# One stretch of whole-array products in each expert round, weights of the second block in pairs, and the next block's first chunk later in the queue

## The chip, the cores and the metric

The kernel runs on one core of one Trainium2 chip. The metric is the time of one execution on the device in microseconds (us), as the median of several runs; a lower time is better. The engines are named as in the profile: PE is the matrix engine (PEld its weight loads), DVE, ACT and POOL are the vector, scalar and general engines, and SP issues the DMA transfers.

## The reference

A sequence of 256 tokens of width 1024 goes through a first block of two layers and then a second block of one layer, all in 32-bit floating point. Of the first block, the part that matters here is the mixture of experts at the end of each layer: each token is sent to two of 32 experts, and each expert is a small gated network.

```python
def first_block(x, ...):
    for l in range(2):
        x = x + mixer(rms_norm(x, attn_norm[l])) @ w_out[l]       # mLSTM, attention, gating
        x = x + hier_moe(rms_norm(x, ffn_norm[l]), ..., w1[l], w3[l], w2[l])

def expert_block(rows, rw, e):              # inside hier_moe, for each expert e
    xi = x_pad[rows]                        # its tokens
    h = silu(xi @ w1[e]) * (xi @ w3[e])     # 1024 -> 256, twice
    return (h @ w2[e]) * rw                 # 256 -> 1024, added back to the tokens

def second_block(x, ...):
    proj = rms_norm_2(x, norm_w) @ w_in_2   # 1024 -> 6144: two attentions, gates
    ...
    return x + y @ w_out_2
```

## The kernel before

The 256 tokens stay in the core's memory; nearly all traffic is weights. A queue of weight tiles of 128 x 2048 (1 MB each) is written out by hand at L237 to L262, and SP issues it strictly in that order. A tile is issued when the program hands back a buffer (`done` at L214, which calls `pump` at L174). During the expert stage 19 buffers of other uses are lent to the queue, and at its end (`reclaim`, L201) only five remain.

An expert's weights are three tiles: "first thirds" and "second thirds" hold w1 and w3 for the two halves of the 1024 input features, and "third matrices" hold w2. The 32 experts are dealt with in 11 rounds: rounds 0, 1 and 4 to 7 have two experts of 64 token places each, the others four experts of 32 places. A round's products use the array in two or four column groups, one for each expert, which can run at the same time: `hidden` (L1127) has 8 steps, `outp` (L1163) has 4, and one step is one product for each of the round's experts. These are called tiled products below. Each of them stands in the trace as two records, since the data is 32-bit.

The other products of a round use the whole array of 128 columns: `gather` (L1108) picks the tokens of the next two rounds and scales them into X (32 products, evicted by ACT at L1122 through the two PSUM buffers called "a"; the two halves of one buffer hold two eviction groups of four products), `gates` (L1089), `turn` (L1146, the transposes of a round's hidden values and its place matrix) and `combine` (L1184, adds a round's output to the token sums, four products for each half n). `gather` and `gates` run in odd rounds, for the two rounds that follow.

Who follows whom in the program of round i: `hidden(i)`, in whose middle (`mid_way`, L1243) stand `combine(i-2, 1)` and `turn(i-1)`; then the two halves of `outp(i-1)`, and in odd rounds a half of the gather behind each of them (`prepare_four`, L1191). A planner turns the program into one order for each engine: at each moment of its own model of time it takes the earliest instruction of the program that is ready. So an instruction whose PSUM buffer or weights are late by that model is overtaken by later ones, and the order on PE in the trace is mixed.

At the end of a layer the first weight chunk of the next block stands eight places before the end of the layer's tiles (L254), ahead of the third matrices of rounds 9 and 10; it is split into a high and a low half by ACT and DVE (`prepare`, `split`, L266 to L274) after `hidden(10)`. The last four tiles arrive in halves (L189 to L197).

In the second block `tok512` (L1381) multiplies the tokens with 512 columns of weights as two chunks of 256 columns, each over all 1024 features: three products for each of 8 feature groups and 2 token groups (`tokm`, L470, and `mm3`, L457).

Of the kernel before, what the change touches and what calls it, by code (L numbers as in the profile page):

```python
# [45 lines left out]
for _c in W_IN_CHUNKS:  # L46
    W_IN_OFF.append(W_IN_OFF[-1] + _c)


# [58 lines left out]
def block_kernel(ctx: ExitStack, tc: tile.TileContext, A, out):  # L108
# [48 lines left out]
    def acc():  # L157
        return mm("acc")
# [78 lines left out]
    for l in range(L):  # L237
        ex = []
        rounds = [ROUNDS[i][1] for i in LOADS]
        for now, before in zip(rounds + [[]], [[]] + rounds):  # L240
            for c in range(2):
                ex.extend(chunk_of(l, e, c) for e in now)
            ex.extend(chunk_of(l, e, 2) for e in before)
        ex.insert(BRIEF, ex.pop(3))
        for i in range(len(W_IN_CHUNKS)):
            a, b = W_IN_OFF[i], W_IN_OFF[i + 1]
            if l == 0 or i:
                queue.append((("in", l, i), A["w_in"][l][:, 8 * a:8 * b]))
            if i == 1:
                queue.append((("u", l), A["w_u"][l]))  # L250
            if i in EARLY:
                queue.append(ex.pop(0))
        queue.extend((("out", l, i), A["w_out"][l][:, i * 2048:(i + 1) * 2048]) for i in range(4))
        ex.insert(len(ex) - 8, following(l + 1))  # L254
        queue.extend(ex)
# [228 lines left out]
    def chunks(key, k):  # L484

        prepare(key)
        i = split_keys.index(key) + 1
        if i < len(split_keys) and split_keys[i] in loaded and split_keys[i][:2] == key[:2]:
            prepare(split_keys[i])
        return [t.rearrange("p (k c) -> p k c", k=k) for t in ready.pop(key)]  # L490

    def mixer(l):
# [584 lines left out]
    def experts(l, xh, xl, whl, slot, wg, perms, P0, mci):  # L1077
# [29 lines left out]

        def gather(q, k2s=range(4)):  # L1108

            P = Ps[q]  # L1110
            n = P.shape[2]
            for k2 in k2s:
                ps = mm("a").rearrange("p (a b) -> p a b", a=2)
                for a in range(2):
                    k = 2 * k2 + a
                    i = 0
                    for t in (xh, xl):
                        for j in range(2):
                            nc.tensor.matmul(ps[:, a, :n], t[:, j, k * 128:(k + 1) * 128], P[:, j], start=i == 0,  # L1119
                                             stop=i == 3)  # L1120
                            i += 1
                    nc.scalar.activation(X[:, k, :n], ps[:, a, :n], AF.Identity, bias=0.0, scale=g[:, k:k + 1])  # L1122

        def keys(i):
            return [[("e", l, e, c) for c in range(3)] for e in ROUNDS[i][1]]

        def hidden(i, mid_way):  # L1127
            q, p = divmod(i, 2)
# [3 lines left out]
            for k in range(8):  # L1132
# [4 lines left out]
                if k == 3:  # L1137
                    done(*[x[0] for x in kk_])
                    mid_way()
            done(*[x[1] for x in kk_])  # L1140
# [21 lines left out]

        def outp(i, between):  # L1163
            nonlocal yhl
# [5 lines left out]
            for n in range(2):  # L1170
# [8 lines left out]
                if n:  # L1179
                    done(*[x[2] for x in kk_])  # L1180
                    combine(i, 0)
                between(n)

        def combine(i, n):  # L1184
            PT = hs[i][1]
            for t in range(2):
                for j in range(2):
                    nc.tensor.matmul(po[j][n], PT[:, j * 128:(j + 1) * 128], yhl[:, n, t],  # L1188
                                     start=i == 0 and t == 0, stop=i == NR - 1 and t == 1)

        def prepare_four(q, n):  # L1191
            if n:
                gates(q)
            gather(q, (2 * n, 2 * n + 1))

# [7 lines left out]
        warm(3)  # L1203
        prepare_four(0, 0)
        prepare_four(0, 1)

# [33 lines left out]
        for i in range(NR):  # L1240
            q, p = divmod(i, 2)
            last = 2 * q + 2 >= NR
            def mid_way():  # L1243
                if i > 1:
                    combine(i - 2, 1)
                if i:
                    turn(i - 1)
                (arrange_places, arrange_weights, lambda: None)[min(i, 2)]()
                if i == NR - 2:
                    add_plain()  # L1250

            hidden(i, mid_way)
            if i == NR - 1:
                reclaim()
                prepare(following(l + 1)[0])
                x = big("x", [128, 2, D], name="x")
            if p == 0 and not last:
                onehot(q + 1)
            if i:
                outp(i - 1, (lambda n: prepare_four(q + 1, n)) if p and not last else lambda n: None)  # L1260
        combine(NR - 2, 1)
        most = nc.values_load(mci[0:1, 0:1], min_val=0, max_val=1 << 14)
        tc.no_sync_barrier()
        tc.mark_branch_hint_location(f"fits{l}", hint=0, engines=[mybir.EngineType.PE])
        turn(NR - 1)
        outp(NR - 1, lambda n: None)
        take_x(po, 0)
# [95 lines left out]
    def second():  # L1363
# [17 lines left out]
        def tok512(i, dst):  # L1381
            for c in range(2):
                w = win2(i + c)
                ps = acc().rearrange("p (a b) -> p a b", a=2)
                tokm(ps, hT, w, 256)
                for j in range(2):
                    copy_scaled(dst[:, j, c * 256:(c + 1) * 256], ps[:, j], r[:, j:j + 1])

# [207 lines left out]
def pack(I):  # L1596
# [71 lines left out]
    A["vec2"] = v2  # L1668
    A["w_in_2"] = c(kp(f(I["w_in_2"])[0]).reshape(128, 8, 24, 256).transpose(2, 0, 1, 3).reshape(24, 128, 2048))
    for n, s in (("w_up_a", "w_up_moba_2"), ("w_up_b", "w_up_sb_2")):  # L1670
# [19 lines left out]
```

## Time and profile before

| | before |
|---|---|
| median of 3 runs | 961.7 us (960.76 to 962.31) |
| the profiled execution | 966.68 us, span 964.9 us |
| PE busy | 938.3 us, 97% of the span |
| expert stage of layer 0, of layer 1 (first gather to the last combine) | 154.8 to 376.5 us, 515.3 to 735.2 us |
| moved from memory | 271.27 MB read, 284 GB/s over the span |

The profile is of one execution; its span runs from the first to the last instruction. A busy PE says only that some product was in flight: a product on one column group alone counts like one on all four. DMA shares are of the core's 16 DMA engines.

### The profile page before, as it was taken

Reading aid. Unit: us, or ns where it says so; the run is one execution under the profiler, and the core shown is the slowest. Engines: PE = TensorE matmul, PEld = TensorE weight load, DVE = VectorE, ACT = ScalarE, POOL = GpSimd, SP = SyncE. Lnnn points to the kernel's source line nnn. Section 1 sums busy time; section 2 is a strip of 40 time slices with the busy share of each in tenths; the row PEclk is TensorE's granted clock in tenths of the full one; section 3 lists DMA queues with packets and bytes.
Section 4 is the critical chain, followed back from the end, with each engine's and each line's share of the span. In section 5 each row is a group of like instructions: output and inputs, shape, how many; then the busy total and the mean of one; then the engine's idle time right before and its main releaser. Section 6 shows DMA issues by size and latency. Waiting matters only on the chain.

```text
span 964.9 us, 14997 instructions
## 1 busy us (share of the span) xinstructions
PE 938.3 (97%) x5834; PEld 622.2 (64%) x5834; DVE 466.2 (48%) x1121; ACT 380.4 (39%) x714; POOL 20.3 (2%) x60
## 2 busy tenths in 40 slices
PE   8989999999999999999999999999998999999998
PEld 6878875433244335889885433344335988899996
DVE  5698665211111115688665211111115777786574
ACT  5576442212122015585542212122125446845442
POOL 0100000000000000300000000000000000000000
PEclk9999999999999999999999999999999999999999
DMA  9537467999999999437568899999999542155531
GB/s 355 181 131 288 160 256 286 369 367 420 421 422 420 397 418 366 126 133 283 185 236 303 352 392 422 420 420 421 416 418 365 181 155 102 45 175 177 186 119 43
DMA packets 42589, 273.38 MB, mean 283 GB/s; under 512 B 5256, under 2 KB 7440, under 8 KB 12048
## 3 DMA queue, kind: packets, MB, share of 16 engines
q1 hardware_dynamic: 40160, 268.48, 70.9%
q10 hardware_dynamic: 2352, 3.87, 1.3%
q8 instruction: 49, 0.80, 0.3%
q14 instruction: 28, 0.23, 0.1%
HBM read 271.27 MB, written 2.63 MB: 284 GB/s over the span
## 4 chain that ended last, share of the span: by engine, by line
PE 80%; DVE 7%; DMA 7%; ACT 5%; issue 1%; SPq 0%; DVEq 0%; ACTq 0%
PE mm L1135 18%; PE mm L459 10%; PE mm L460 10%; PE mm L461 10%; PE mm L1174 10%; PE mm L1119 6%; PE mm L1188 4%; DMA w<-in_w_e 3%; DMA w<-in_w_in 3%; DVE wlo L273 2%; ACT whi L272 1%; PE mm L571 1%; PE mm L576 1%; PE mm L689 1%; DMA x<-in_x 1%
## 5 line engine op out<-in xcount | busy, mean ns | idle before, releaser
L1135 PE MATMUL mm<-w,X 128*32 128x512 f32 (+1 forms) x1024 | 191.1, 598 | 2.0 <-DMA w<-in_w_e 2.0
L273 DVE TENSOR_TENSOR wlo<-w,whi 128x1024 fp32r<-128x1024 f32 (+3 forms) x124 | 145.3, 1183 | 26.4 <-ACT whi L272 26.3
L272 ACT ACTIVATE whi<-w 128x1024 fp32r<-128x1024 f32 (+3 forms) x124 | 122.2, 1016 | 72.8 <-issue 42.4
L1174 PE MATMUL mm<-w,ehT 128*32 128x512 f32 (+1 forms) x512 | 132.8, 600 | 1.0 <-ACT ehT L1158 1.0
L459 PE MATMUL mm<-hT,whi 128*128 128x256 f32 (+2 forms) x432 | 125.4, 290 | 0.2 <-ACT whi L272 0.2
L461 PE MATMUL mm<-hT,wlo 128*128 128x256 f32 (+2 forms) x432 | 124.6, 288 | 0.8 <-DVE wlo L273 0.8
L460 PE MATMUL mm<-lT,whi 128*128 128x256 f32 (+2 forms) x432 | 124.6, 288 | 0.0
L1135 PEld LDWEIGHTS mm<-w,X 128*32 128x32 f32 (+1 forms) x1024 | 48.2, 119 | 94.5 <-issue 83.6
L460 PE MATMUL mm<-wlo,hT 128*128 128x256 f32 x288 | 83.9, 291 | 1.1 <-DVE wlo L273 1.1
L459 PE MATMUL mm<-whi,hT 128*128 128x256 f32 x288 | 84.6, 294 | 0.1
L461 PE MATMUL mm<-whi,lT 128*128 128x256 f32 x288 | 83.5, 290 | 0.0
L459 PEld LDWEIGHTS mm<-hT,whi 128*128 128x128 f32 (+2 forms) x432 | 80.7, 187 | 2.3 <-issue 0.8
L460 PEld LDWEIGHTS mm<-lT,whi 128*128 128x128 f32 (+2 forms) x432 | 80.6, 187 | 1.8 <-issue 1.3
L461 PEld LDWEIGHTS mm<-hT,wlo 128*128 128x128 f32 (+2 forms) x432 | 80.6, 187 | 1.7 <-DVE wlo L273 1.5
L1122 ACT ACTIVATE X<-mm,vec 128x256 f32<-128x256 f32 (+1 forms) x96 | 43.3, 455 | 93.4 <-PE mm L1119 92.5
L1178 DVE TENSOR_TENSOR yhl<-mm,yhl 128x512 fp32r<-128x512 f32 x44 | 30.2, 691 | 90.1 <-ACT yhl L1177 90.1
L1174 PEld LDWEIGHTS mm<-w,ehT 128*32 128x32 f32 (+1 forms) x512 | 31.5, 119 | 61.9 <-issue 55.2
L1143 DVE SCALAR_TENSOR_TENSOR eh<-eh,mm 128x256 f32<-128x256 f32 x22 | 9.3, 421 | 108.0 <-ACT eh L1142 108.0
L1119 PEld LDWEIGHTS mm<-P,xh 128*128 128x128 f32 x192 | 29.3, 188 | 49.2 <-ACT X L1122 32.5
L1160 DVE TENSOR_SCALAR ePT<-mm,C 128x256 fp32r<-128x256 f32 x22 | 10.6, 484 | 100.8 <-ACT ehT L1158 100.8
L460 PEld LDWEIGHTS mm<-wlo,hT 128*128 128x128 f32 x288 | 55.5, 193 | 2.9 <-DVE wlo L273 1.5
L1142 ACT ACTIVATE eh<-mm,gt 128x256 f32<-128x256 f32 x22 | 10.4, 474 | 118.1 <-PE mm L1135 118.1
(460 smaller groups left out, 1485.2 us busy)
## 6 DMA issues: line engine op xcount, KB each, us to landing
w<-in_w_e SPq DMA_DIRECT2D x184, 1024.0 KB, 12.7
w<-in_w_in SPq DMA_DIRECT2D x37, 1024.0 KB, 4.9
w<-in_w_out SPq DMA_DIRECT2D x12, 1024.0 KB, 4.9
w<-in_w_e SPq DMA_DIRECT2D x16, 512.0 KB, 9.0
w<-in_w_in SPq DMA_DIRECT2D x4, 768.0 KB, 4.2
w<-in_w_up_a SPq DMA_DIRECT2D x2, 1024.0 KB, 4.8
w<-in_w_up_b SPq DMA_DIRECT2D x2, 1024.0 KB, 4.8
w<-in_w_u SPq DMA_DIRECT2D x2, 960.0 KB, 10.9
```

Of the source, the lines that this page charges most:

```text
L272: nc.scalar.activation(hi[:, s_], w[:, s_], AF.Copy)
L273: nc.vector.tensor_sub(lo[:, s_], w[:, s_], hi[:, s_].bitcast(F32))
L459: nc.tensor.matmul(ps, st[0], mv[0], start=first, stop=False)
L460: nc.tensor.matmul(ps, st[0], mv[1], start=False, stop=False)
L461: nc.tensor.matmul(ps, st[1], mv[0], start=False, stop=last)
L1119: nc.tensor.matmul(ps[:, a, :n], t[:, j, k * 128:(k + 1) * 128], P[:, j], start=i == 0, stop=i == 3)
L1122: nc.scalar.activation(X[:, k, :n], ps[:, a, :n], AF.Identity, bias=0.0, scale=g[:, k:k + 1])
L1135: nc.tensor.matmul(ph[w * a:w * a + w], X[:, k, c0:c0 + w], take(kk_[a][k // 4])[:, (k % 4) * 512:(k % 4 + 1) * 512], start=k == 0, stop=k ...
L1160: nc.vector.tensor_scalar(PT, pT[:, 256:], cc("place" if w == 64 else "place32"), None, op0=OP.is_equal)
L1174: nc.tensor.matmul(py[w * a:w * a + w], hT[:, c * 128 + w * a:c * 128 + w * a + w], take(kk_[a][2])[:, n * 1024 + c * 512:n * 1024 + (c + ...
L1178: nc.vector.tensor_sub(yhl[:, n, 1], py, yhl[:, n, 0].bitcast(F32))
L1188: nc.tensor.matmul(po[j][n], PT[:, j * 128:(j + 1) * 128], yhl[:, n, t], start=i == 0 and t == 0, stop=i == NR - 1 and t == 1)
```

## The change

In the expert stage, `mid_way` and `prepare_four` go. The program of round i becomes `hidden(i)` without an interruption, `outp(i-1)` without one, and then all whole-array products in one go: `combine(i-1, 0)` (inside `outp`), `turn(i)`, in odd rounds the whole of `gather` and `gates`, and `combine(i-1, 1)`. `gather` takes its PSUM buffers in turn from "b" and "a", four in all, and in all gathers but a layer's first the second half of each buffer is evicted by DVE in place of ACT. The queue takes the next block's first chunk four places from the end of the layer's tiles: behind the third matrices of round 9 and ahead of those of round 10. In the second block `tok_pair` takes two chunks as two halves of the features for all 512 columns, and each product is 512 columns wide, into two PSUM buffers.

```diff
-        ex.insert(len(ex) - 8, following(l + 1))
+        ex.insert(len(ex) - 4, following(l + 1))
...
+    def tok_pair(hT, first, second):
+        ps = [acc() for j in range(2)]
+        for half, key in enumerate((first, second)):
+            w = chunks(key, 4)
+            for k in range(4):
+                for j in range(2):
+                    mm3(ps[j], [t[:, 4 * half + k, j * 128:(j + 1) * 128] for t in hT], [t[:, k] for t in w],
+                        half == 0 and k == 0, half == 1 and k == 3)
+        return ps
...
-        def gather(q, k2s=range(4)):
+        def gather(q):
...
-            for k2 in k2s:
-                ps = mm("a").rearrange("p (a b) -> p a b", a=2)
+            for k2 in range(4):
+                ps = mm("baba"[k2]).rearrange("p (a b) -> p a b", a=2)
...
-                    nc.scalar.activation(X[:, k, :n], ps[:, a, :n], AF.Identity, bias=0.0, scale=g[:, k:k + 1])
+                    if a and q:
+                        nc.vector.tensor_scalar(X[:, k, :n], ps[:, a, :n], g[:, k:k + 1], None, op0=OP.mult)
+                    else:
+                        nc.scalar.activation(X[:, k, :n], ps[:, a, :n], AF.Identity, bias=0.0, scale=g[:, k:k + 1])
...
-            def mid_way():
-                if i > 1:
-                    combine(i - 2, 1)
-                if i:
-                    turn(i - 1)
-                (arrange_places, arrange_weights, lambda: None)[min(i, 2)]()
-                if i == NR - 2:
-                    add_plain()
-
-            hidden(i, mid_way)
+            hidden(i)
             if i == NR - 1:
                 reclaim()
                 prepare(following(l + 1)[0])
                 x = big("x", [128, 2, D], name="x")
+
+            if i:
+                outp(i - 1)
+            if i < NR - 1:
+                turn(i)
+            (arrange_places, arrange_weights, lambda: None)[min(i, 2)]()
             if p == 0 and not last:
                 onehot(q + 1)
+            if i == NR - 2:
+                add_plain()
+            if p and not last:
+                gather(q + 1)
+                gates(q + 1)
             if i:
-                outp(i - 1, (lambda n: prepare_four(q + 1, n)) if p and not last else lambda n: None)
-        combine(NR - 2, 1)
+                combine(i - 1, 1)
...
         def tok512(i, dst):
-            for c in range(2):
-                w = win2(i + c)
-                ps = acc().rearrange("p (a b) -> p a b", a=2)
-                tokm(ps, hT, w, 256)
-                for j in range(2):
-                    copy_scaled(dst[:, j, c * 256:(c + 1) * 256], ps[:, j], r[:, j:j + 1])
+            for j, ps in enumerate(tok_pair(hT, ("in2", i), ("in2", i + 1))):
+                copy_scaled(dst[:, j], ps, r[:, j:j + 1])
```

## Rows read from the trace of the kernel before

**Rows 1.** The page: slices of 24 us, granted PE clock and DMA share, in tenths

```profile
PEclk9999999999999999999999999999999999999999
DMA  9537467999999999437568899999999542155531
```

**Rows 2.** Windows, layer 0: stretch, length, busy PE, PEld, DVE, ACT, POOL, clock, DMA share, GB/s

```profile
182.00:192.00 10.00, 10.00 (x54) 5.51 (x52) 1.68 (x8) 3.32 (x8) 0.00 (x0) 1.00 0.92 344
192.00:198.00 6.00, 6.00 (x47) 2.27 (x50) 1.10 (x3) 0.86 (x2) 0.00 (x0) 1.00 0.52 171
...
215.00:310.00 95.00, 95.00 (x416) 38.19 (x409) 16.66 (x42) 20.76 (x42) 0.00 (x0) 1.00 1.01 421
310.00:325.00 15.00, 15.00 (x92) 4.56 (x90) 2.96 (x7) 2.31 (x5) 0.00 (x0) 1.00 0.96 376
```

**Rows 3.** Windows, layer 1, the same columns

```profile
545.00:553.00 8.00, 8.00 (x50) 4.49 (x52) 1.55 (x7) 2.75 (x6) 0.00 (x0) 1.00 0.85 295
553.00:560.00 7.00, 7.00 (x62) 2.47 (x54) 1.15 (x3) 0.54 (x2) 0.00 (x0) 1.00 0.69 238
```

**Rows 4.** Waits of SP's queue between 186 and 197 us: total, times, longest

```profile
SPq L191 <- PE mm L1135: 6.6, 1, 6.6
```

**Rows 5.** Timeline of PE, part of round 1: start, length, line, shapes, records

```profile
180.70 0.50 PE L1119 MATMUL mm<-P,xh 128*128 128x256 f32 x2
...
181.37 1.07 PE L1174 MATMUL mm<-w,ehT 128*64 128x512 f32 x2
182.37 0.51 PE L1119 MATMUL mm<-P,xh 128*128 128x256 f32 x2
...
183.51 1.08 PE L1174 MATMUL mm<-w,ehT 128*64 128x512 f32 x4
184.53 0.50 PE L1119 MATMUL mm<-P,xh 128*128 128x256 f32 x2
```

**Rows 6.** Waits of the engines over the whole span: total, times, longest

```profile
PEld mm L1119 <- ACT X L1122: 32.5, 44, 0.8
```

**Rows 7.** Timeline of PE, round 7, where nothing is gathered

```profile
282.99 3.60 PE L1174 MATMUL mm<-w,ehT 128*64 128x512 f32 x16
286.52 1.20 PE L1188 MATMUL mm<-yhl,ePT 128*128 128x512 f32 x4
287.65 3.65 PE L1135 MATMUL mm<-w,X 128*64 128x512 f32 x16
```

**Rows 8.** Timeline of PE: first and last of eleven tiled stretches before 194.0 us

```profile
158.09 1.07 PE L1135 MATMUL mm<-w,X 128*64 128x512 f32 x2
...
192.03 2.77 PE L1135 MATMUL mm<-w,X 128*32 128x512 f32 x22
```

**Rows 9.** Groups by line and shape: count, busy us, mean ns, idle before

```profile
L1122 ACT ACTIVATE X<-mm,vec 128x256 f32<-128x256 f32 x80 | 37.4, 473 | 73.4 <-PE mm L1119 72.5
```

**Rows 10.** SP's transfer of the next chunk at 334.8 us: issue, time to landing

```profile
L191 SPq DMA_DIRECT2D w<-in_w_in x1: 429/429/429, 334.8 to 334.8; - x1
...
DMA to landing us min/median/max: 16.7/16.7/16.7
```

**Rows 11.** Timeline, end of layer 0

```profile
363.00 1.99 ACT L272 ACTIVATE whi<-w 128x1024 fp32r<-128x1024 f32 x2
...
372.48 0.16 PEld L1174 LDWEIGHTS mm<-w,ehT 128*32 128x32 f32 x8 [0.93 <-SPq L1276]
```

**Rows 12.** Timeline of PE: products of 256 and of 512 columns, a wait in the second block

```profile
741.03 0.38 PE L448 MATMUL mm<-C,x 128*128 128x128 f32 x2 [1.75 <-DVE lT L455]
...
891.02 0.28 PE L459 MATMUL mm<-hT,whi 128*128 128x256 f32 x1
891.14 0.28 PE L460 MATMUL mm<-lT,whi 128*128 128x256 f32 x1
...
945.05 0.39 PE L459 MATMUL mm<-whi,yh 128*128 128x512 f32 x1
945.28 0.39 PE L460 MATMUL mm<-wlo,yh 128*128 128x512 f32 x1
```

**Rows 13.** Timeline of PE, round 9: the output products of four experts

```profile
337.80 1.04 PE L1174 MATMUL mm<-w,ehT 128*32 128x512 f32 x2
...
347.42 3.62 PE L1174 MATMUL mm<-w,ehT 128*32 128x512 f32 x20
```

More of the change, by code (lines that the diff above doesn't have):

```diff
@@ L47 @@
     W_IN_OFF.append(W_IN_OFF[-1] + _c)
+PAIRS, PAIRS2 = (2, 8), (0, 2, 4, 12)
 VC = dict(attn=0, ffn=8, mix=16, conv_w=24, conv_b=56, gate=64, aq=66, akv=68, qh=69, kh=70, bs=71)
@@ L1121, in gather, with hidden @@
                             i += 1
-                    nc.scalar.activation(X[:, k, :n], ps[:, a, :n], AF.Identity, bias=0.0, scale=g[:, k:k + 1])
+                    if a and q:
+                        nc.vector.tensor_scalar(X[:, k, :n], ps[:, a, :n], g[:, k:k + 1], None, op0=OP.mult)
+                    else:
+                        nc.scalar.activation(X[:, k, :n], ps[:, a, :n], AF.Identity, bias=0.0, scale=g[:, k:k + 1])
         def keys(i):
             return [[("e", l, e, c) for c in range(3)] for e in ROUNDS[i][1]]
-        def hidden(i, mid_way):
+        def hidden(i):
             q, p = divmod(i, 2)
@@ L1138, in hidden @@
                     done(*[x[0] for x in kk_])
-                    mid_way()
             done(*[x[1] for x in kk_])
@@ L1161, in turn, with outp @@
             hs[i] = hT, PT
-        def outp(i, between):
+        def outp(i):
             nonlocal yhl
@@ L1181, in outp @@
                     combine(i, 0)
-                between(n)
         def combine(i, n):
@@ L1189, in combine @@
                                      start=i == 0 and t == 0, stop=i == NR - 1 and t == 1)
[L1191 to L1194, printed above, removed]
         slotT = small([NE, 2, 256], BF, name="slotT")
@@ L1203, in experts @@
         warm(3)
-        prepare_four(0, 0)
-        prepare_four(0, 1)
+        gather(0)
+        gates(0)
         def arrange_places():
@@ L1265, in experts @@
         turn(NR - 1)
-        outp(NR - 1, lambda n: None)
+        outp(NR - 1)
         take_x(po, 0)
@@ L1668, in pack @@
     A["vec2"] = v2
-    A["w_in_2"] = c(kp(f(I["w_in_2"])[0]).reshape(128, 8, 24, 256).transpose(2, 0, 1, 3).reshape(24, 128, 2048))
+    w2 = kp(f(I["w_in_2"])[0])
+    A["w_in_2"] = c(w2.reshape(128, 8, 24, 256).transpose(2, 0, 1, 3).reshape(24, 128, 2048))
+    for i in PAIRS2:
+        for h in range(2):
+            A["w_in_2"][i + h] = w2[:, 4 * h:4 * h + 4, 256 * i:256 * i + 512].reshape(128, -1)
     for n, s in (("w_up_a", "w_up_moba_2"), ("w_up_b", "w_up_sb_2")):
```

## The prediction

> **What bounds the kernel now.** I began with the slices of the page [rows 1]: the granted clock stays at its upper level (2.4 GHz), and in the two expert stages the DMA share stands at nine tenths or more for nine and eight slices on end, as it does nowhere else for long. PE is shown as busy there too, so the next view is the one by windows. From 215 to 310 us the share is 1.01 at 421 GB/s [rows 2]; more than that the queue does not move anywhere, so I take 1.01 as full. One tile of 1 MB then takes 1.05 MB / 421 GB/s = 2.49 us. Ahead of that the queue is not full: 0.92 and 0.52 in layer 0 [rows 2], 0.85 and 0.69 in layer 1 [rows 3]. Against 1.01 this is 10 x 0.09 + 6 x 0.49 = 3.8 us of lost transfer in layer 0, and 8 x 0.16 + 7 x 0.32 = 3.5 us in layer 1. SP has one wait of 6.6 us there, for `hidden` on PE [rows 4]: the buffers that it needs are those of round 2's first thirds, which `hidden(2)` gives back in its middle, at 194.0 us. So PE is the bound up to about 200 us of a layer, and the queue behind that. At the end PE's weight load at 372.48 us has waited 0.93 us [rows 11]; the engine named had nothing left to do that this load needs, and the late thing there is the second halves of the last tiles. The stage ends when the queue has delivered, and what is gained on PE behind 200 us only counts if the queue was started earlier.
>
> **What a broken stretch costs.** In rows 5, one product on a single column group (two records) takes from 181.37 to 182.37, 1.00 us; one on both groups (four records) takes 1.02 us from 183.51. Four full steps take 3.53 us from 282.99 [rows 7]. So a tiled step costs 0.84 us, and 0.17 us is paid for each stretch; a partner left behind costs a whole step more. Four whole-array products take 0.67 us from 180.70 and eight take 1.14 us from 182.37 [rows 5]: 0.12 each and 0.20 for each stretch. One more change to and fro costs 0.17 + 0.20 = 0.37 us.
> Why it is broken: PE never does the second four products of a PSUM buffer right behind the first four; it does four, goes elsewhere, does eight, goes elsewhere [rows 5], and its weight loads for the gather wait for ACT's evictions 44 times, 32.5 us in all [rows 6]. One eviction takes 0.473 us [rows 9], four products 0.47 us. With two buffers PE runs out of first halves after 0.94 us, less than it takes to finish the first eviction and hand the buffer back. With four it has 1.9 us of first halves ahead, and the second halves go to DVE.
>
> **The early part of a stage.** From 158.09 to 194.01 us, 35.9 us, I count eleven tiled stretches [rows 8], together 25.0 us, and ten whole-array ones between them, 10.9 us. Of the latter 10 x 0.20 = 2.0 us is the price of entering, so 8.9 us is products. After the change the same point, half of `hidden(2)`, needs 8 + 8 + 4 + 4 = 24 full steps, 20.2 us, in five stretches (four, and one cut where `turn(0)` finds its values ready): + 0.85 us. Whole-array: 8.9 us; + 1.5 us, since `combine(0, 1)` (1.13 us from 286.52 [rows 7], less 0.2 for the entry) and `turn(1)` (some 0.55 us with its small products) now lie ahead of that point; + 4 x 0.20. Together 20.2 + 0.85 + 8.9 + 1.5 + 0.8 = 32.3 us, 3.6 us sooner. The third matrices of round 0 come free some 7 us sooner, as `outp(0)` no longer waits between pieces of the gather. DVE's four evictions in a gather, and `arrange_places` and `arrange_weights`, which move to the end of rounds 0 and 1, stand beside tiled products; uncovered they would cost one eviction's 0.47 us a gather.
> The queue so starts its full stretch 3.6 us sooner in layer 0, and 3.5 us in layer 1, where no more was lost. Behind it PE must keep the lead up to the point where the 19 buffers are full and the share dips again (0.96 from 310 to 325 us [rows 2]); odd rounds like that of rows 5 lose several changes at 0.37 us and lone steps at 0.84 us, which PE gets back there. Even rounds [rows 7] have little to give. What PE gains beyond the queue's lead is wait.
> **Sum for the expert stages: 7.1 us**; bounds 0 (the queue is as late as before) and 3.8 + 15 x 0.05 + 3.5 = 8.1 us.
>
> **The chunk that moves.** It is issued at 334.83 and lands 16.7 us later, at 351.5 [rows 10]; its split starts at 363.00 [rows 11]. Four places later in the queue are four tiles, 10.0 us: it would land at 361.5, or 357.9 with the lead. SP passes nothing else, and the four third matrices of round 9 land 2.5 us sooner each. The split stays covered by 1.5 to 5 us: nothing. Uncovered, ACT's 1.99 us and about half as much on DVE stand ahead of the next block's first product: up to 3.2 us a layer.
>
> **The pairs.** Products of 256 columns follow each other at 0.12 us, those of 512 at 0.227 us on average over that stretch (0.23 in the two shown) [rows 12]. Four pairs have 4 x 96 products now: 46.1 us; then 4 x 48: 43.6 us. That is 2.5 us, on PE's path, as PE is busy nearly throughout the second block. The evictions are wider by 256 columns, twice in place of four times; the next pair's products hide them, and the last pair's lie beside attention work. At the block's beginning PE waits 1.75 us for `lT` [rows 12], because one feature group covers only 6 x 0.12 us; it will cover 6 x 0.227. I take 1.0 us of the wait, bounds 0 and 1.75.
> The Trainium skill ("TensorE: Matmul & The Clock Gate", section "Wait — 56ns, not 53.3ns?") has a product cost its columns at 2.4 GHz and a fixed 2.5 ns; by that the pairs would save 192 x 2.5 ns = 0.5 us, and the trace, with 13 ns for each product saved, does not agree.
>
> **The forecast** is 7.1 + 2.5 + 1.0 = 10.6 us. The profiled execution took 966.68 us, so its like would take 956.1; the median of the runs lies 5.0 us below it, and from there it is 961.7 - 10.6 = **951.1 us**. All bounds together give 8.1 + 2.5 + 1.75 = 12.4 us, 949.3, and 2.5 us if only the pairs work. I go down to 946 at the low end, since `hidden(2)` may come earlier than I count and layer 1's stage end has slack of its own.
>
> **Rivals.**
> *The stretch stays broken.* The order on PE is the planner's, and whatever weights or buffers its model holds for late are overtaken as before. Then the queue is as late as now and only the second block gains: 3.5 us, **958.2**. For it: lone products like those of rows 13 are dealt out where the planner holds weights for late, which the change does not speed up. Against it: those of rows 5 lie where weights were there, and what they wait for is the buffer. A buffer that two engines may not touch at once is what the Trainium skill describes ("PSUM — Partial Sum Buffer", section "PSUM bank collisions raise a hardware error"); rows 5 and 6 agree.
> *Slower: a faster PE starves, and the planner deals out lone products.* In round 9 the output products of four experts run partly alone, 1.0 us a step, before a full stretch of 20 records in 3.6 us [rows 13]: 12 of the 32 records are in lone steps of one product each, 6 x 1.0 us where nothing more would be needed, so some 6 us are lost in one such round. Once PE is ahead of the queue in the planner's model, every round of four experts can be dealt out so, and on the chip, where the weights had long landed, PE becomes the bound. Three such rounds more in a layer cost 18 us; less the 3.6 us and some 8 us from two odd rounds, 6.4 us a layer are left: 961.7 + 12.8 - 3.5 = **971**. It decides from the second such round in a layer on.
> *The pairs give 0.5 us* (a fixed cost per product that is small): **953.1**. The spacing of rows 12 speaks against it.
> *The chunk is late* in addition: up to 6.4 us on top of the forecast, **957.5**.
>
> **How the numbers follow.** Forecast 0.58, stretch still broken 0.18, starved and slower 0.13, pairs at 0.5 us 0.04, late chunk 0.07. The range takes all but the slower rival and the edge of the second: 946 to 961. About 0.2% (1.9 us) is what a measurement of this kernel can tell from no change. Above 0.2% faster are all but the slower rival and a third of the second: 0.81. Within: 0.06. Slower: 0.13.
>
> **What would show it.** Right: between 182 and 204 us the DMA share is 0.95 or more; SP's wait of 6.6 us is shorter by more than half; the gathers are single stretches of 32 products in about 4 us; 512-column products at 0.227 us in the second block's first 20 us; the second layer begins 3 to 4 us earlier, the second block 7. Wrong: the DMA share is full earlier and yet the layer ends no earlier (then PE had become the bound, and lone tiled products between 215 and 360 us would show it), or the dip at 310 us grows, or PE waits for the chunk's split at the head of a block.

## The result, and the profile after

| | before | changed |
|---|---|---|
| median, range (6 executions each) | 961.7 us, 960.8 to 962.6 | 956.0 us, 954.7 to 958.4 |
| ratio, 95% interval | | 0.9936, 0.9920 to 0.9953 |
| second comparison (26 and 8 executions) | 962.3 us | 957.5 us; ratio 0.9944, 0.9923 to 0.9965 |
| profiled execution, its span | 966.7, 964.9 us | 954.7, 952.8 us |

The change makes the kernel faster, by 5.7 us and by 4.7 us at the median in the two comparisons. The forecast was 951.1 us, 10.6 us faster: the direction and the place were right, the size was almost twice too large. The executions of one kernel fall into two groups some 4 us apart (in the second comparison 18 of before's lie between 960.4 and 962.8 us and eight between 964.0 and 966.7), so a median also moves with how many fall into each.

The two profiles cut into stages (first block up to the first gather product; expert stage from there to the last product of the last sum; mixer; the same again; then the second block's end), all from the timelines of PE:

| us | first block | expert stage, layer 0 | mixer | expert stage, layer 1 | rest |
|---|---|---|---|---|---|
| before | 154.8 | 221.7 | 138.8 | 219.9 | 229.7 |
| changed | 151.9 | 217.2 | 138.8 | 217.8 | 227.2 |

The first block is no part of the change. PE does the same products in the same order in it in all kernels of this study, and yet the profiles show from 150.3 to 154.8 us for it (more on that at the end). So the 12 us between the two profiled executions are not all the change's; 2.9 us of them lie ahead of it.

The slices of the changed kernel's page (granted clock and DMA share in tenths), against [rows 1]:

```profile
PEclk8999999999999999999999999999999999999999
DMA  9537567899999998347558899999999632245531
```

Layer 0 by windows (stretch, length, busy PE, PEld, DVE, ACT, POOL, clock, DMA share, GB/s), against [rows 2]:

```profile
172.00:182.00 10.00, 10.00 (x56) 5.34 (x53) 3.53 (x11) 2.90 (x6) 0.00 (x0) 1.00 1.01 420
182.00:192.00 10.00, 10.00 (x87) 5.09 (x89) 3.27 (x15) 1.31 (x3) 0.00 (x0) 1.00 0.68 257
192.00:198.00 6.00, 6.00 (x35) 2.34 (x28) 2.28 (x4) 1.72 (x4) 0.00 (x0) 1.00 1.01 422
...
215.00:310.00 95.00, 94.33 (x471) 39.71 (x470) 22.73 (x55) 15.56 (x31) 0.00 (x0) 1.00 1.01 421
310.00:325.00 15.00, 15.00 (x95) 5.43 (x92) 2.27 (x5) 1.58 (x3) 0.00 (x0) 1.00 1.01 422
```

The same of layer 1, against [rows 3]:

```profile
535.00:545.00 10.00, 10.00 (x81) 6.80 (x84) 4.54 (x22) 2.54 (x6) 0.00 (x0) 1.00 0.83 351
545.00:552.00 7.00, 7.00 (x52) 1.97 (x44) 1.59 (x3) 1.07 (x2) 0.00 (x0) 1.00 0.82 286
```

In layer 0 the queue is full from 192 us on and stays so through 325 us, where it dipped before. But the hole ahead of it is still there: 10 x 0.33 = 3.3 us of lost transfer between 182 and 192 us, and 10 x 0.18 + 7 x 0.19 = 3.1 us in layer 1. SP's queue between 170 and 200 us (total, times, longest), against [rows 4], says why:

```profile
SPq L194 <- PE mm L1152: 18.5, 6, 10.1
```

It waits 10.1 us for `hidden(2)`, longer than the 6.6 us of before. The wait ends at 189.3 us, when about half of the products of `hidden(2)` are done and the first buffer of round 2's first thirds comes back. I call this point the middle, and count it from the stage's first gather product: 37.4 us here, 39.2 us before. PE's timeline in that stretch (start, length, line, shapes, records, idle time before it and its releaser), against [rows 5] and [rows 8]:

```profile
156.63 1.07 PE L1152 MATMUL mm<-w,X 128*64 128x512 f32 x2
...
158.30 7.95 PE L1152 MATMUL mm<-w,X 128*64 128x512 f32 x36
167.01 0.41 PE L1167 MATMUL mm<-C,eh 128*128 128x128 f32 x2 [0.76 <-DVE eh L1160]
...
177.66 1.19 PE L1203 MATMUL mm<-yhl,ePT 128*128 128x512 f32 x4
...
185.62 7.07 PE L1152 MATMUL mm<-w,X 128*32 128x512 f32 x64
```

From 177.66 to 185.62 us PE is in one stretch of whole-array products: the gather of round 1 is whole, as it was meant to be. Of a layer's six gathers only those of rounds 1 and 5 are. The first one has one lone product in it, and those of rounds 3, 7 and 9 still have one to three tiled stretches between their products and last 10 to 15 us; they lie behind the middle. Ahead of the whole stretch stand a product on one column group alone (156.63) and a wait of 0.76 us for DVE ahead of `turn(0)` (167.01). Over the whole span PE's weight loads for the gather now wait little for ACT (total, times, longest), against [rows 6], and 1.6 us in 4 times for DVE:

```profile
PEld mm L1133 <- ACT X L1139: 6.1, 14, 0.8
```

And behind the hole PE has become the one that waits, for weights:

```profile
205.51 1.91 PE L1152 MATMUL mm<-w,X 128*32 128x512 f32 x2 [2.11 <-DMA w<-in_w_e]
```

### The profile page after: what moved, and what is told of

Its sections match the earlier page's. It is cut to its first block, busy times and chain, and to the rows that moved or that the text cites. A ratio compares the mean times of both kernels' runs of the same rounds, so it can differ in the third digit from the quotient of the medians.

```text
span 952.8 us, 14653 instructions
## 1 busy us (share of the span) xinstructions
PE 916.8 (96%) x5642; PEld 606.7 (64%) x5642; DVE 483.3 (51%) x1157; ACT 361.9 (38%) x670; POOL 18.7 (2%) x60
## 4 chain that ended last, share of the span: by engine, by line
PE 74%; DMA 14%; DVE 6%; ACT 3%; issue 1%; SPq 0%; ACTq 0%; DVEq 0%
PE mm L1152 14%; PE mm L463 11%; PE mm L462 10%; PE mm L464 10%; DMA w<-in_w_e 10%; PE mm L1190 8%; PE mm L1133 5%; PE mm L1203 3%; DMA w<-in_w_in 3%; DVE wlo L276 2%; PE mm L585 1%; DMA masks<-in_consts 1%; PE mm L590 1%; ACT whi L275 1%; PE mm L703 1%
## 5 line engine op out<-in xcount | busy, mean ns | idle before, releaser
L1152 PE MATMUL mm<-w,X 128*32 128x512 f32 (+1 forms) x1024 | 172.5, 599 | 5.5 <-DMA w<-in_w_e 5.5
L1190 PEld LDWEIGHTS mm<-w,ehT 128*32 128x32 f32 (+1 forms) x512 | 33.6, 119 | 81.7 <-issue 62.0
L1158 ACT ACTIVATE eh<-mm,gt 128x256 f32<-128x256 f32 x22 | 10.4, 473 | 180.7 <-PE mm L1152 180.7
L463 PE MATMUL mm<-wlo,hT 128*128 128x256 f32 (+1 forms) x224 | 72.4, 323 | 1.8 <-DVE wlo L276 1.8
L462 PE MATMUL mm<-whi,hT 128*128 128x256 f32 (+1 forms) x224 | 73.2, 327 | 0.0
L464 PE MATMUL mm<-whi,lT 128*128 128x256 f32 (+1 forms) x224 | 72.0, 321 | 0.0
L1193 ACT ACTIVATE yhl<-mm 128x512 fp32r<-128x512 f32 x44 | 26.3, 598 | 99.1 <-PE mm L1190 99.1
L1203 PE MATMUL mm<-yhl,ePT 128*128 128x512 f32 x176 | 52.6, 419 | 0.0
L463 PEld LDWEIGHTS mm<-wlo,hT 128*128 128x128 f32 x224 | 42.7, 190 | 6.6 <-DVE wlo L276 2.9
L1133 PE MATMUL mm<-P,xh 128*128 128x256 f32 (+1 forms) x192 | 42.6, 303 | 3.9 <-ACT X L1139 1.9
```

The costliest lines, as they stand in the source:

```text
L462: nc.tensor.matmul(ps, st[0], mv[0], start=first, stop=False)
L463: nc.tensor.matmul(ps, st[0], mv[1], start=False, stop=False)
L464: nc.tensor.matmul(ps, st[1], mv[0], start=False, stop=last)
L1152: nc.tensor.matmul(ph[w * a:w * a + w], X[:, k, c0:c0 + w], take(kk_[a][k // 4])[:, (k % 4) * 512:(k % 4 + 1) * 512], start=k == 0, stop=k ...
L1158: nc.scalar.activation(h, ph[:, :256], AF.Tanh, scale=gts[q][:, p, 1:2])
L1190: nc.tensor.matmul(py[w * a:w * a + w], hT[:, c * 128 + w * a:c * 128 + w * a + w], take(kk_[a][2])[:, n * 1024 + c * 512:n * 1024 + (c + ...
```

## The experiments

My theory: each expert stage ends a fixed time after `hidden(2)`'s middle, since from there the DMA queue runs without a hole; whatever PE gains later is wait. The rivals: PE's own work is what counts wherever it lies, or the gain is the second block's.

The trace shows directly that the end hangs on the queue. In layer 1 it has the landing of the last half tile in every profile, and the stage ends 4.1 us behind it in twelve of the thirteen (4.4 us in before's). In the changed kernel this half tile is issued at 711.33 us and lands at 721.5; the stage ends at 725.6:

```profile
DMA to landing us min/median/max: 10.2/10.2/10.2
```

**e0, the changed kernel again.** 

> The changed kernel once more, beside the three single parts on the same chip: 956.0 us, 5.7 us under before. If the parts add up, the gains of the rounds alone, the pairs alone and the chunk alone make this sum; if the rounds alone give 3.2 and the pairs 2.5, the chunk gives nothing. In its profile the expert stages last 217.2 and 217.8 us and hidden(2)'s middle lies 37.4 us behind the stage's first gather (39.2 before).

Measured 957.5 us (median of 8), 0.9944 of before. Stages 218.6 and 217.2 us, middle at 37.4 us.

**e1, the rounds alone.** The new order of the rounds, the four buffers and the two evicting engines; the second block's chunks and the place of the next chunk as before:

```
-        ex.insert(len(ex) - 4, following(l + 1))
+        ex.insert(len(ex) - 8, following(l + 1))
...
-            for j, ps in enumerate(tok_pair(hT, ("in2", i), ("in2", i + 1))):
-                copy_scaled(dst[:, j], ps, r[:, j:j + 1])
+            for c in range(2):
+                w = win2(i + c)
```

> The changed order of the rounds alone (single stretches, four PSUM buffers, two evicting engines), without the pairs and with the chunk where it was before. Theory (the DMA queue's run of full transfer begins with hidden(2)'s middle, and the stage ends when the queue has delivered): the two expert stages are as short as in the changed kernel's profile, 217.2 and 217.8 us (first gather to last sum; before 221.7 and 219.9), and the second block is as long as before, 229.7 us. The time is 2.5 us above the changed kernel's 956.0: 958.5, that is 3.2 us under before. Rival (the rounds bring nothing that lasts, the whole gain is the second block's): 961.7. Rival (the moved chunk is part of the gain, since third matrices land sooner): 959.5 to 961.

Measured 956.8 us, ratio 0.9948 (0.9928 to 0.9967). The rounds alone give what the whole change gives (e0, 957.5 us), within the interval; I had expected them 2.5 us slower than the whole. Stages 217.9 and 218.3 us, the last one 228.5.

**e2, the pairs alone.**

```
-            for c in range(2):
-                w = win2(i + c)
...
+            for j, ps in enumerate(tok_pair(hT, ("in2", i), ("in2", i + 1))):
+                copy_scaled(dst[:, j], ps, r[:, j:j + 1])
```

> The pairs alone: four pairs of the second block's weight chunks with products of 512 columns, all else as before. Theory: 192 products fewer at 13 ns each save 2.5 us, and nothing else moves: second block 227.2 us, expert stages 221.7 and 219.9 as before, time 959.2. If the wait of 1.75 us at the block's beginning goes as well and is not found again behind: 958.2 (which I priced at 1.0 us). Rival, worked out from the fixed cost per product of the Trainium skill ("TensorE: Matmul & The Clock Gate", section "Wait — 56ns, not 53.3ns?"): 0.5 us, 961.2.

Measured 963.5 us, ratio 1.000 (0.9984 to 1.0017): no gain, and 2.5 us, let alone 3.5, is outside the interval. In its profile the last stage lasts 227.1 us against 229.7, and the two expert stages together are 0.3 us longer than before's, so this one profile shows 2.4 us of gain behind the first block, which the runs do not show. At the block's beginning the wait of [rows 12] is not gone. It has another name (same columns as above):

```profile
741.04 0.40 PE L460 MATMUL mm<-whi,hT 128*128 128x512 f32 x1 [1.06 <-ACT hT L455]
741.27 0.40 PE L461 MATMUL mm<-wlo,hT 128*128 128x512 f32 x1
741.51 0.39 PE L462 MATMUL mm<-whi,lT 128*128 128x512 f32 x1
```

The products of 512 columns follow each other at 0.23 us, as I had taken from another stretch.

**e3, the chunk alone.**

```
-        ex.insert(len(ex) - 8, following(l + 1))
+        ex.insert(len(ex) - 4, following(l + 1))
```

> The next block's first chunk alone four places later in the queue, all else as before. Theory: its split stays covered, as it lands at 361.5 us and is split from 363.0 on, and the last four tiles land as before: 961.7, within 0.5. Rival (cover gone): ACT's split of 1.99 us and half as much on DVE stand ahead of the next block's first product, up to 3.2 us a layer: 965 to 968. Rival (the four third matrices that now go first feed PE 2.5 us sooner and PE is the bound at that point): 957 to 960.

Measured 964.4 us, ratio 1.0008 (0.9991 to 1.0025): nothing. Its split starts at 366.1 us in place of 363.0 and is still over before the next block begins at 376.

**e4, the gather on two buffers.** Everything else as changed:

```
-                ps = mm("baba"[k2]).rearrange("p (a b) -> p a b", a=2)
+                ps = mm("a").rearrange("p (a b) -> p a b", a=2)
```

> The changed kernel with the gather on two PSUM buffers instead of four (its evictions are dealt out between ACT and DVE as in the changed kernel). Theory: PE runs out of first halves after 0.94 us, so the gather is broken into pieces again, hidden(2)'s middle comes 1 to 2 us later than the 37.4 us (behind the stage's first gather) of the changed kernel, the DMA queue's run of full transfer begins as much later in each layer, and the time is 2 to 4 us above the changed kernel's 956.9 (the median of its 14 executions so far): 959 to 961. Rival (one whole stretch comes from the rewritten order of the rounds alone): gathers of about 4 us in one piece, 956.9.

Measured 959.4 us, ratio 0.9963 (0.9946 to 0.9979), 2.5 us above the changed kernel's 956.9. The gather is in pieces again, with `hidden(2)` dealt out between them. PE's timeline in e4:

```profile
183.83 1.05 PE L1152 MATMUL mm<-w,X 128*32 128x512 f32 x2
...
185.95 1.06 PE L1152 MATMUL mm<-w,X 128*32 128x512 f32 x8
...
188.09 1.07 PE L1152 MATMUL mm<-w,X 128*32 128x512 f32 x8
...
191.76 4.49 PE L1152 MATMUL mm<-w,X 128*32 128x512 f32 x38
```

The middle comes at 39.2 us, as late as before. So the buffers carry the 1.8 us. What e4 keeps against before (2.9 us by the medians) has, in its profile, 1.6 us in layer 0's stage (219.8 against 221.4) and 2.0 in the last one (227.7 against 229.7).

**e7 and e8, the same extra work at two places.** Four products on `X`, whose result nothing uses, once ahead of `hidden(2)` and once ahead of `hidden(6)`:

```
+        def extra(n):
+            ps = mm("a")
+            for _ in range(n):
+                nc.tensor.matmul(ps, X[:, 0, :128], X[:, 0:2].rearrange("p a b -> p (a b)"), start=True, stop=True)
...
         for i in range(NR):
...
+            if i == 2:
+                extra(4)
```

> The changed kernel with four whole-array products (fp32, 512 columns, about 0.85 us each, 3.4 us together) put on PE in each layer right ahead of hidden(2); nothing uses their result. Theory (the end of a stage hangs on hidden(2)'s middle, which lets the queue go on): each expert stage becomes 3 to 3.4 us longer, the time 956.9 + 6 to 6.8 = 963 to 964. Rival (PE's time before 200 us of a layer is covered, since the queue catches up later): 957 to 958.

> The same 3.4 us of products in each layer, put right ahead of hidden(6), in the stretch in which the queue is full. Theory (behind 200 us of a layer PE's time is covered by the queue, so that what PE gains there is only wait): 0 to 1 us a layer, 957 to 959, and PE's waits for DMA at the stage's end get shorter. Rival (PE is the bound there in the changed kernel): 3.4 us a layer, 963 to 964.

e7 took 964.5 us, ratio 1.0023 (1.0003 to 1.0043): 7.6 us above the changed kernel. e8 took 958.1 us, ratio 0.9957 (0.9937 to 0.9977): 1.3 us above it. The timelines of e7 and, second, of e8 show the same piece of work on PE:

```profile
183.85 3.60 PE L1202 MATMUL mm<-X 128*128 128x512 f32 x8
187.38 7.07 PE L1152 MATMUL mm<-w,X 128*32 128x512 f32 x64
```

```profile
268.93 3.60 PE L1202 MATMUL mm<-X 128*128 128x512 f32 x8
```

In e7 the middle moves from 37.4 to 40.8 us and the stages from means of 217.9 and 217.8 to 221.9 and 221.1 us; in e8 they are 218.0 and 218.2 us. In layer 0 of e8 the queue is full in the very stretch with the extra work (windows):

```profile
215.00:310.00 95.00, 94.01 (x478) 40.75 (x478) 22.42 (x54) 15.50 (x31) 0.00 (x0) 1.00 1.01 421
```

So 3.5 us of PE's time cost 3.3 to 4 us a layer ahead of `hidden(2)` and 0.2 to 0.5 us behind it. This is the test that tells the theory from the rival. (Some of the totals is another thing: e7's last stage is 231.5 us long, with 6.8 us at 1.2 GHz from 736.6 us on, where PE stands in a wait of 2.9 us; e8's is 229.1 us.) One thing that I had expected of e8 did not come: PE's waits for weights are not shorter (5.7 us over the span against 5.5). In layer 0's stage PE is idle for 7.9 us in place of 8.3, while the tiled products behind the middle take 121.6 us in place of 123.6. So the slack that PE has there lies less in idle time than in the way the planner deals out the tiled products.

**e9 and e13, `hidden(2)` sooner.** Round 0's sums and the gates of group 1 wait until round 2's products are out:

```
             done(*[x[1] for x in kk_])
+            if i == 2:
+                gates(1)
+                combine(0, 0)
+                combine(0, 1)
...
-                gates(q + 1)
-            if i:
+                if i > 1:
+                    gates(q + 1)
+            if i > 1:
                 combine(i - 1, 1)
```

> The changed kernel with round 0's sums (both halves of combine(0)) and the gates of group 1 moved from round 1 to behind round 2's first products. Theory: hidden(2)'s middle comes some 2 us sooner than 37.4 us behind the stage's first gather, the queue starts as much sooner where it still has a gap (2.3 and 2.5 us), and each layer ends 1.5 to 2 us sooner: 953 to 954. Rival (the end of a stage no longer hangs on that point, but on PE's order at its end): 956.9.

> e9 once more, beside e10 and e11 on the same chip: 954.6 us, with hidden(2)'s middle 35.9 us behind the first gather and expert stages of 215.6 to 216.3 us.

954.6 us, ratio 0.9911 (0.9880 to 0.9941), and on the second occasion 953.2 us, ratio 0.9900 (0.9878 to 0.9922): faster than both kernels, by 7.7 and 9.0 us at the median against before, and by 2.3 and 3.7 against the changed kernel's 956.9 from the earlier occasions. The middle comes at 35.8 us in both; the stages last 216.3 and 215.6 us, then 216.3 and 215.7. The hole of layer 0 has shrunk to 10 x 0.15 us (window of e9):

```profile
180.00:190.00 10.00, 10.00 (x81) 3.96 (x80) 2.15 (x9) 1.12 (x3) 0.00 (x0) 1.00 0.86 338
```

Some 2 us of products were moved (seven of 0.23 us and the gates) and 1.5 us gained, because without those fillers `hidden(2)` is dealt out into the gather again (timeline of e9):

```profile
179.94 1.05 PE L1152 MATMUL mm<-w,X 128*32 128x512 f32 x2
...
182.55 1.06 PE L1152 MATMUL mm<-w,X 128*32 128x512 f32 x8
...
184.21 6.21 PE L1152 MATMUL mm<-w,X 128*32 128x512 f32 x54
```

**e10, half of that.** As e9, with `combine(0, 0)` left ahead of the gather (its line is not in the added block, and the condition at its call is not there).

> As e9, but of round 0's sums only the second half (combine(0, 1)) moves behind round 2's first products, with the gates; the first half stays ahead of the gather. Theory (each layer's stage lasts 180.4 us from hidden(2)'s middle on, as in the five profiles so far): the middle comes 36 to 36.5 us behind the first gather (35.9 in e9, 37.4 in the changed kernel), each stage lasts 216.4 to 216.9 us, the time is between e9 and the changed kernel: 955 to 956. Rival (e9's gain came from something else, for instance the sums' own place beside tiled work): no fixed relation to the middle.

Measured 957.3 us, ratio 0.9931 (0.9905 to 0.9956), 1.3 us above what I had said. The middle came at 36.8 us, later than I said, as one lone product of `hidden(2)` still stands in the gather; the stages are 217.6 and 217.1 us. The relation holds, the guess of the middle missed by 0.3 to 0.8 us. That the median is no better than the changed kernel's is more than the stages explain; in the profile the first block lasts 154.7 us, and whether the other executions had the same is not known.

The relation over all profiles (middle: SP's issue that ends the wait for `hidden(2)`, from the first gather product on; mean of both layers, which agree within 0.1 us):

| | middle | stage, layer 0 and 1 | stage less middle |
|---|---|---|---|
| before (and e2, e3: the same order of the rounds) | 39.2 | 221.2 to 221.7; 219.2 to 220.7 | 182.2; 180.8 |
| changed (and e0, e1) | 37.4 | 217.2 to 218.6; 217.2 to 218.3 | 180.5; 180.4 |
| e4 | 39.2 | 219.8; 219.7 | 180.6; 180.4 |
| e7 | 40.8 | 221.9; 221.1 | 181.1; 180.3 |
| e8 | 37.4 | 218.0; 218.2 | 180.7; 180.9 |
| e9, e13 | 35.8 | 216.3; 215.6 | 180.5; 179.8 |
| e10 | 36.8 | 217.6; 217.1 | 180.8; 180.2 |
| e11 (below) | 35.8 | 215.8; 216.7 | 179.9; 180.8 |

Five microseconds of difference in the middle, and behind it 179.8 to 181.2 us in every single stage of the new order, within one kernel as between kernels (the changed kernel's two profiles have 179.8 and 181.2 in layer 0). The old order has 180.0 to 181.5 us in layer 1; only its layer 0 lies apart, at 182.0 to 182.5.

**e11, e9 without the pairs.** The same lines as in e1's second edit.

> As e9, but without the pairs (the second block's weights as before). Theory, as the pairs alone gave nothing that could be measured and 0.45 us behind the block's first 6 us in their profile: 0 to 1.5 us slower than e9 (954.6), 955 to 956. Rival (the pairs give their 2.5 us of products wherever the block's start does not take it back): 957.

Measured 956.2 us, ratio 0.9930 (0.9908 to 0.9952), against e13's 953.2 on the same chip: 3.0 us by the medians, though the two intervals overlap (against e9's 954.6 it is 1.6), while e2 says 0.0 against before. In the two profiles the last stage is 228.7 us without and 227.5 us with the pairs. From the starts of one product to the next, added up: the pairs' products take 50.9 us without and 48.5 us with them (both with the waits below), the 768 other products with 256 columns 95.6 and 96.3 us, small products 32.4 and 32.9. So 2.4 us are saved and 1.2 us come back in the same block. More than half of these 1.2 us lie with the 768 products: nearly all of them are followed by the next start after 0.12 us, but with the pairs 42 and without them 35 only after more than 0.16 us. The waits at the block's beginning, e11 and then e13:

```profile
727.62 0.28 PE L463 MATMUL mm<-wlo,hT 128*128 128x256 f32 x1 [0.95 <-issue]
```

```profile
731.01 0.50 PE L463 MATMUL mm<-wlo,hT 128*128 128x512 f32 x1 [0.23 <-DVE wlo L276]
...
734.40 0.51 PE L463 MATMUL mm<-wlo,hT 128*128 128x512 f32 x1 [0.60 <-DVE wlo L276]
```

## Why the prediction was right in kind and too large

**The bound: right.** The queue is what ends the stage, and PE's time behind 200 us of a layer is covered by it: e8 against e7. The mark that I gave for it was wrong, though. SP's wait was to become shorter by half; it grew from 6.6 to 10.1 us, and the share between 182 and 204 us is not 0.95 throughout, but 0.68 up to 192 and 1.01 from there. SP came to it sooner (the two tiles ahead went out at 176.9 and 178.1 us, before at 184.6 and 186.3), and only its end counts. The sign of single gathers of about 4 us held for two gathers of six, and the one that counts is among them.

**The early part: the term that was mis-sized.** I had `hidden(2)`'s middle 3.6 us sooner; it is 1.8 us sooner, in both layers and in all three profiles of the new order. Counted from the first gather product, my working was 14.5 us of whole-array products (3.3 ahead of 158.09 us, then 8.9 + 1.5 + 0.8) and 21.1 us of tiled ones. The changed kernel's timeline has 14.3 and 22.4 us, and a wait of 0.76 us. The whole-array part was right. (With the two small products at 165.56 us counted, the trace of before has twelve tiled stretches and eleven between them, not eleven and ten, so that the entries cost 2.2 us and not 2.0; put right, my working would have come to 3.8 us.) The tiled part has one lone product more (1.0 us, at 156.63), the step "five stretches" counted none; and the step "one cut where `turn(0)` finds its values ready" is where the wait stands: the values are not ready when PE gets there. The chain from `hidden(0)` to these values, one instruction on ACT and two on DVE, takes 1.4 us in both kernels. Before, PE went on with `hidden(1)` and came to `turn(0)` 1.9 us behind the end of the chain; now it stops for `turn(0)` after three products of `hidden(1)`, 0.76 us too soon. The chain's last instruction and `turn(0)` before, and then the chain's last instruction in the changed kernel (its `turn(0)` is at 167.01, above):

```profile
170.60 0.48 DVE L1144 SCALAR_TENSOR_TENSOR eh<-eh,gt,mm 128x256 f32<-128x256 f32 x1
172.93 0.44 PE L1151 MATMUL mm<-C,eh 128*128 128x128 f32 x2
```

```profile
166.38 0.48 DVE L1160 SCALAR_TENSOR_TENSOR eh<-eh,gt,mm 128x256 f32<-128x256 f32 x1
```

**What follows from it: 7.1 us forecast, 5.7 us in the profiles.** Means of three profiles each: layer 0 from 221.4 to 217.9 us, layer 1 from 220.0 to 217.8. In layer 1 the 2.2 us are the 1.8 us and little else. In layer 0 half is the middle. Of the other 1.7 us, what I had taken as a condition is worth 15 x 0.05 = 0.75 us: the dip at 310 us [rows 2] is gone, 0.96 to 1.01. The rest, about 1 us, is not settled; two profiles of the changed kernel differ by 1.4 us in this stage. So layer 0 reached its 3.5 us in part by another way than I said, and that this lies next to the 3.6 of the forecast is luck.

**A broken stretch.** e4 undoes one line of the change and the middle is back at 39.2 us, so the number of buffers is shown to be the reason. That ACT's evictions need DVE's help is not: e4 keeps the two evicting engines and is broken all the same, and four buffers with ACT alone were not tried.

**The chunk: nothing, as said.** e3, and in the changed kernel's timeline the split is over 11 us ahead of the next block's first product at 369.86:

```profile
356.52 2.00 ACT L275 ACTIVATE whi<-w 128x1024 fp32r<-128x1024 f32 x2
```

**The pairs: 3.5 us forecast; 0 to 1.5 by three views, 3.0 by one.** The 2.5 us of products are right: 2.4 us between e11 and e13, and in the changed kernel the spacing that [rows 12] had in another stretch:

```profile
745.68 0.39 PE L463 MATMUL mm<-wlo,hT 128*128 128x512 f32 x1
745.91 0.39 PE L464 MATMUL mm<-whi,lT 128*128 128x512 f32 x1
```

What failed is "on PE's path, as PE is busy nearly throughout", and the 1.0 us of the wait. The wait does not go, it changes its place and its name. In the four profiles without pairs it is 1.75, 1.32, 0.63 and 0.95 us; in seven with pairs it is 0.67 (the changed kernel) to 1.58 us (e0), and 2.9 and 2.5 us in e7 and e8. PE is through the first chunk and then stands before the second chunk's split on DVE:

```profile
735.53 0.50 PE L463 MATMUL mm<-wlo,hT 128*128 128x512 f32 x1 [0.24 <-DVE wlo L276]
...
738.74 0.50 PE L463 MATMUL mm<-wlo,hT 128*128 128x512 f32 x1 [0.43 <-DVE wlo L276]
```

Over all profiles but e7's the last stage is 229.2 us long without pairs (four of them) and 227.7 with (eight), 1.5 us apart. By the runs it is 0.0 (e2), nothing (e0 lies 0.8 us above e1) and 3.0 us (e11 against e13); these scatter too much to choose between 0 and 3. In part the gain comes back where products of the block follow each other less closely (e11); why the planner's order has more such places with the pairs is not settled.
The Trainium skill ("TensorE: Matmul & The Clock Gate", section "Wait — 56ns, not 53.3ns?"), with its fixed 2.5 ns for a product, gave an estimate of 0.5 us for the pairs. Three of the four views come nearer to that than to my 3.5 us, but not for that reason: the trace has 0.120 us for 256 columns and 0.227 for 512, so 13 ns are saved for each product, and the block gives part of them back.

**The offset.** I took 5.0 us off since before's profiled execution lies that far above its median. The study's profiles show where 4.5 of them can lie: in the first block, which lasts 154.8 us there and 150.3 in e13, with the same products. No execution of before near its median was profiled, so this is argued.

**The sum.** 5.7 + 1.5 = 7.2 us by the profiles, and 5.7 and 4.7 by the medians, whose intervals reach from 3.4 to 7.7 us. The two agree within these. The changed kernel's executions show a lower mean granted clock (0.992 to 0.994 against 0.997 of before), which would act in this direction. In the expert stages it costs nothing: e9 has 3.4 us at 1.2 GHz from 206.8 us on, e13 has none, and layer 0's stage lasts 216.3 us in both. That it costs the difference elsewhere is argued, not shown.

**The rivals.** The stretch that decides is not broken; of the four gathers behind it in a layer three are. The slower rival showed itself in part: PE waits for weights at 205.5 us, and in round 9 12 of 32 records still stand in lone steps, as before [rows 13]. The last of them and the full stretch:

```profile
331.83 1.90 PE L1190 MATMUL mm<-w,ehT 128*32 128x512 f32 x4
...
336.39 3.62 PE L1190 MATMUL mm<-w,ehT 128*32 128x512 f32 x20
```

But with the queue full to the end of the layer PE's time there is covered (e8), which is why the rival did not decide.

## What to carry to other kernels

Where a queue ends the stage, find the one release that lets it run without a hole, and count everything up to that point product by product, with the lone steps and the waits that the faster order will meet; what is saved behind it is worth next to nothing (3.5 us more there cost 0.2 to 0.5). A wait that ends at an engine's chain does not shrink because its consumer is faster: look what the chain itself needs (1.4 us here), and what the consumer does meanwhile. And before two profiles are subtracted, compare a stage that the change does not touch.

## What was not expected of the hardware

The first block's products have the same order in all kernels, and its length scattered by 4.5 us between the profiles (150.3 to 154.8). Windows of e10 and then of e13 (stretch, length, busy PE, PEld, DVE, ACT, POOL, clock, DMA share, GB/s):

```profile
12.00:17.00 5.00, 5.00 (x23) 4.54 (x23) 4.49 (x11) 3.53 (x8) 0.00 (x0) 1.00 1.02 422
...
90.00:100.00 10.00, 8.91 (x52) 7.59 (x52) 9.54 (x22) 3.65 (x6) 0.00 (x0) 0.83 0.98 385
```

```profile
12.00:17.00 5.00, 5.00 (x44) 5.00 (x44) 4.46 (x12) 3.25 (x8) 0.00 (x0) 1.00 1.03 427
...
90.00:100.00 10.00, 8.91 (x60) 7.48 (x59) 9.31 (x21) 2.92 (x7) 0.00 (x0) 1.00 0.91 338
```

In e10 the granted clock is at 1.2 GHz for 3.4 us from 95.7 us on, which cost 1.6 us by the starts of the same products; in e13 it stays at 2.4 GHz, with the same busy time of PE in that window and the same waits of PE ahead of it (0.4 and 0.6 us). The other 2.9 us are lost ahead of 18 us; between 12 and 17 us e10 does 23 products and e13 44. There the clock column says 1.00 for both, but the products themselves do not. Timelines of e10 and then of e13:

```profile
14.26 0.42 PE L462 MATMUL mm<-hT,whi 128*128 128x256 f32 x1
14.47 0.41 PE L463 MATMUL mm<-lT,whi 128*128 128x256 f32 x1
...
17.25 0.29 PE L464 MATMUL mm<-hT,wlo 128*128 128x256 f32 x1
17.37 0.29 PE L462 MATMUL mm<-hT,whi 128*128 128x256 f32 x1
```

```profile
13.02 0.28 PE L463 MATMUL mm<-lT,whi 128*128 128x256 f32 x1
13.14 0.28 PE L464 MATMUL mm<-hT,wlo 128*128 128x256 f32 x1
```

0.21 us from one to the next in e10 until 17.0 us, 0.12 in e13: e10's PE is at about half its rate there. The column does not show it because it has nothing to show: the trace's records of the clock begin at 17.2 us in e10 and at 5.7 us in e13, and the column fills the time ahead of them with 1.00. All profiles begin at the lower rate, with eight products of 512 columns 0.43 us apart from 1.0 us on; then come transposes as `x` lands, in both alike. Before, e2, e3 and e10 show the late rise (154.6 to 154.8 us for the block); e1, e7, e9, e11 and e13 the early one (150.3 to 151.0); the changed kernel, e0, e4 and e8 lie between (151.6 to 152.0 us, with 6.8 us at 1.2 GHz in the column, from 7 us on). All three profiles of the old order of the rounds are among the late ones, and one of ten of the new order. With one profile for each kernel it is not shown whether the edit has a part in this.
